# Rotation tables pinned behind the token factor, their loads cut in two, a norm weight moved into its weights, and one product group reordered

## The chip, the cores and the metric

One NeuronCore of a Trainium2 chip runs the kernel. The metric is the device time of one execution in microseconds (us), as the median of several runs. TensorE (PE) multiplies matrices into PSUM banks. VectorE (DVE), ScalarE (ACT) and GpSimd (POOL) do the rest of the arithmetic. SyncE (SP) issues most of the loads and stores (DMAs), POOL some of them. Each engine works through a queue of its own in order; a wait at the head of a queue holds everything behind it.

## What is computed

One decoder layer on 512 tokens of width 1024, all in float32:

```
h  = RMSNorm(x, g_mix);   z = h @ W_in
A  = retention(z) ;  B = 3 groups of dilated window attention(z),
     q and k of each head: RMSNorm with q_gain/k_gain, then rotated by position
x  = x + (sig(g_A) * (A @ W_A) + sig(g_B) * (B @ W_B)) @ W_o
x  = x + relu(RMSNorm(x, g_mlp) @ W_up)^2 @ W_down
x  = x + sig(RMSNorm(x, g_ple) @ W_ple_gate) * (p @ W_ple_proj)
```

The factor of RMSNorm is one number for each token (row) and can be applied after a product; its weight is one number for each column of the left side, that is for each row of the weight matrix.

## The kernel before

**Products in split precision.** Each float32 operand is split into a high part that PE multiplies exactly (hi, made by ACT) and the rest (lo, made by DVE as operand minus hi). A product is three matmuls, hi*hi, hi*lo and lo*hi, into one PSUM bank (`mm3`, L254 to L259). PE therefore has three matmuls of 128x128 by 128x512 for each piece.

**Weights come in units.** `make_plan` (L1088) lists all weights in the order of their use, as units of 512 KB. `fetch` (L179) issues a unit's load on SP into one of six raw buffers; `ahead` (L197) fetches and splits units up to `AHEAD = 2` past those in use, into four pairs of hi and lo buffers; `split_unit` (L214) does the two splits. If a unit has a gain (`g0`), ACT scales by the weight's gain for each row while it makes hi, and DVE makes lo with one scalar_tensor_tensor for each 128 rows; without one, DVE makes it with one subtraction over the whole unit. `units` (L208) hands units to a product.

**The order of the instructions.** The program is traced in the order of the Python code. A scheduler then orders each engine's queue by that order and by times that it assumes for instructions and loads, so an instruction that it takes to be ready early can move ahead of others on its engine. `pin` (L315) ties an instruction behind the one traced before it on the same engine. In the last part of the kernel (`manual_schedule`, L1068 to L1086) ACT and DVE keep the written order. `later` and `tick` (L102, L111) put small work off by a count of product pieces (lag).

**The start.** `setup` (L395) issues the loads of x by columns and of the first four weight units in turn, then of x by rows, then of two more weight units. `load_tables` (L427) then issues the rotation table (`rot_c`, two halves of 512 KB: the first for attention, the second for retention), the attention mask (256 KB) and the q and k gains of all three groups (`rot_gains`, 768 KB, spread over the partitions). `first_panel` (L444) makes q of attention group 0: it splits x and four weight units in turn, then multiplies; in its middle `token_factors` (L503) squares x on ACT, makes v on DVE (L512) and r = v^-0.5 on POOL (L513), and stores r to DRAM and reads it back in another order on SP (L515, L517).

For each of the four tiles of 128 tokens, `consume` (L570) copies the finished bank, times r, to `zn` on ACT (L574), which frees the bank; squares it by heads on ACT (L578), takes a second factor on POOL (L323), applies it on DVE (L580) and rotates (`rotate`, L524) with two table products C and S. `tables` (L555) makes C and S on DVE out of rotation table and gains (L559): two instructions of 128x512 each for q and for k. When four tiles are rotated, PE transposes them by heads (`heads_T`, L545). `embed_operands` (L482) loads p (`praw`) on SP and splits it on ACT (L488) and DVE.

**The MLP.** The hidden width is worked off in four pairs of 512 columns. Each pair's product with `W_down` is a 2x2 block product done with seven block products instead of eight (`seven_gemm`, L923), in the order 4, 3, 5, 4, 3, 5, 2, 2, 1, 1, 7, 7, 6, 6 of half products; each half product uses one unit and takes 12 matmuls. Some units are sums of two weight blocks (a load with an accumulating load on POOL behind it, L194), and the two units of product 1 are differences: DVE subtracts in place (L204) when such a unit is split. The four results are added to x by DVE (`acc`, L945 to L948, line L948) out of the banks; bank 4 is first copied by ACT (L960).

**The embedding gate.** In the last pair, whenever a half of a token tile's x is final (`done`, L950), `gain_T` (L375) multiplies it by `g_ple`, spread over the partitions, on DVE (y, L378), and PE transposes y by four blocks (L333) into a bank; ACT and DVE split that into `h3` hi and lo (L346, L347). When both halves of a tile are there, `mean_squares` (L381) takes its factor, with squares on ACT (L386) and small steps on DVE (L388, L389). Then h3 is multiplied by `W_ple_gate` in two halves of 512 columns, and `fin` (L1077) applies the sigmoid, multiplies by p's projection, adds x and stores.

Of the kernel before, what the change touches and what calls it, by code (L numbers as in the profile page):

```python
# [25 lines left out]
HD = 128  # L26
NG = 3
# [48 lines left out]
class Block:  # L76


    def __init__(self, ctx, tc, a):
        self.tc, self.nc, self.a = tc, tc.nc, a  # L80
        pool = lambda n, b, **k: ctx.enter_context(tc.tile_pool(name=n, bufs=b, **k))
        self.const = pool("const", 1)
        self.wraw = pool("wraw", 6)
        self.wsp = pool("wsp", 4)
        self.bigp = pool("bigp", 16)
        self.tmpp = pool("tmpp", 12)
        self.tabp = pool("tabp", 4)
# [10 lines left out]
        self.hook = None  # L98
        self.plan, self.raws, self.loaded, self.used = [], [], [], 0


# [48 lines left out]

    AHEAD = 2

    def plan_rows(self, w, c0, nk, r0=0):
        for u in range(nk // 2):
            self.plan.append((w[r0 + 256 * u : r0 + 256 * (u + 1), c0 : c0 + 512], None))

    def plan_seven(self, w, r0):


        q = lambda i, j, u: w[r0 + 512 * i + 256 * u : r0 + 512 * i + 256 * (u + 1), 512 * j : 512 * (j + 1)]  # L160
        n = len(self.plan)
        for u in range(2):
            self.plan.append(((q(1, 0, u), q(0, 0, u)), None))
            self.plan.append(((q(0, 1, u), q(1, 1, u)), None))
            self.plan.append((q(1, 1, u), None))
        for u in range(2):
            self.plan.append((q(0, 0, u), None))
        for u in range(2):
            self.plan.append(((None, n + 6 + u, n + 2 + 3 * u), None))
        for u in range(2):  # L170
            self.plan.append(((q(1, 0, u), q(1, 1, u)), None))
        for u in range(2):
            self.plan.append(((q(0, 0, u), q(0, 1, u)), None))
# [23 lines left out]
    def ahead(self, n):  # L197
        while len(self.loaded) < min(len(self.plan), self.used + n):
            i = len(self.loaded)
            self.fetch(i + 1)  # L200
            raw, g0 = self.raws[i]
            src = self.plan[i][0]
            if isinstance(src, tuple) and src[0] is None:
                self.nc.vector.tensor_tensor(raw, raw, self.raws[g0][0], op=ALU.subtract)  # L204
                g0 = None
            self.loaded.append(self.split_unit(raw, g0))

    def units(self, n):  # L208
        self.ahead(n + (0 if self.pinned else self.AHEAD))
# [164 lines left out]

    def gain_T(self, x, t, h, gain, dst, key, lag, bank=None):  # L375

        y = self.tmp("y")
        self.nc.vector.tensor_tensor(y, x[:, h * 512 : (h + 1) * 512], gain[h], op=ALU.mult)  # L378
# [15 lines left out]

    def setup(self):  # L395
        nc, a = self.nc, self.a
        self.gcol = self.const.tile([P, 32], F32, name="gcol")
        nc.scalar.dma_start(self.gcol, a["vec_cols"])
        xr = [self.big("xr") for _ in range(2)]
        self.x_cols = [xr[k // 4][:, k % 4] for k in range(KD)]  # L400
        for u in range(KD // 2):
            src, _ = self.plan[u]
            raw = self.wraw.tile([P, 1024], F32, tag="raw", name=self.nm("raw")).rearrange("p (k n) -> p k n", k=2)
            for k in range(2):
                c = slice((2 * u + k) * P, (2 * u + k + 1) * P)
# [12 lines left out]
        warm = self.tmp("warm")  # L418
        nc.vector.memset(warm, 0.0)
        nc.scalar.activation(warm[:, 500:501], warm[:, 501:502], AF.Copy)  # L420
        wb, wps = warm.bitcast(mybir.dt.bfloat16), self.bank("warm")
        for _ in range(WARM):
            nc.tensor.matmul(wps, wb[:, :P], wb[:, :512], start=True, stop=True)
        self.mhalf = self.const.tile([P, H], F32, name="mhalf")
        nc.gpsimd.memset(self.mhalf, -0.5)

    def load_tables(self):  # L427
        nc, a = self.nc, self.a
        self.rot_c = self.big("rotc")
# [4 lines left out]
        mg = self.big("mg")  # L434
        self.mask = mg[:, 0]
        nc.sync.dma_start(self.mask, a["c_mask"])
        gv = mg.rearrange("p a b -> p (a b)")[:, 512:].rearrange("p (n w) -> p n w", n=4)
        g = a["rot_gains"]
        nc.sync.dma_start(mg.rearrange("p a b -> p (a b)")[:, 512:],
                          bass.AP(tensor=g.tensor, offset=g.offset, ap=[[0, P], [1, 4 * NG * HD]]))  # L440
        self.gains = gv


    def first_panel(self, consume):  # L444
# [110 lines left out]
    def tables(self, g, n):  # L555
        C = self.tabp.tile([P, NT, HD], F32, tag="tab", name=self.nm("C"))
        Sn = self.tabp.tile([P, NT, HD], F32, tag="tab", name=self.nm("S"))
        for o, part, gi in ((C, 0, 2 * n), (Sn, 1, 2 * n + 1)):
            self.nc.vector.tensor_tensor(  # L559
                o, self.rc[:, 0, :, part * HD : (part + 1) * HD],  # L560
                self.gains[:, gi, g * HD : (g + 1) * HD].unsqueeze(1).to_broadcast([P, NT, HD]), op=ALU.mult)
        return C, Sn

    def att_proj(self, g, n):
# [358 lines left out]
    def seven_gemm(self, U, xs, f, ready):  # L923
# [65 lines left out]
    def tail(self, mx):  # L989
# [32 lines left out]
        h3 = None  # L1022
        for f in range(NF // 2):
# [64 lines left out]
    def make_plan(self):  # L1088
# [15 lines left out]
                    self.plan_cols(a["w_up"][0], 512 * (2 * f + b) + 256 * jj, KD)  # L1104
            self.plan_seven(a["w_down"][0], 1024 * f)
        for half in range(2):
            self.plan_rows(a["w_ple_gate"][0], 512 * half, KD)

    def run(self):
        self.w_in = self.a["w_in"][0]  # L1110
        self.make_plan()
        self.setup()
        self.load_tables()
        groups = []
        for g in range(NG):
            groups.append(self.attention(g))
# [7 lines left out]
        assert self.used == len(self.plan) and not self.queue  # L1124


_INS = ["x", "w_in", "g_mlp", "g_ple", "w_ret_out", "w_att_out", "w_o", "w_up", "w_down", "w_ple_proj", "w_ple_gate"]


# [23 lines left out]
```

## Time and profile before

| | |
|---|---|
| median of 3 runs | 1023.94 us (1022.09 to 1024.83) |
| the profiled execution | 1021.85 us |
| its span, first to last instruction | 1020.1 us |
| mean granted PE clock | 0.995 of full speed |
| DMA | 135.37 MB, mean 133 GB/s |

A row of a timeline gives the start and the duration in us, the engine (a q behind it: its queue issues a DMA), the line, the operation, the tile written <- the tiles read, the shape and a count; in brackets stands the engine's idle time before it and what ended it. A row of windows gives for each engine the busy time and (x) the number of instructions; behind them stand the granted PE clock, the share of the DMA engines that was busy and GB/s. A row of waits has who waited <- for whom, then us in total, times and the longest. A row of DMA issues has the count, the size of one and the median us from issue to landing.

### The profile page before, as it was taken

The page shows a single profiled execution, that of the slowest core. Times are in us where ns is not written, and L with a number is a line of the kernel's source. Part 1 is how long each engine was busy: PE and PEld are TensorE (multiplying, and loading weights), DVE is VectorE, ACT ScalarE, POOL GpSimd, SP SyncE. Part 2 cuts the span into 40 slices and gives each one's busy share as a digit, 9 for nine tenths or more (in the row PEclk, how much of TensorE's full clock was granted, in tenths as well). Part 3 has the DMA queues.
Part 4 walks back from the last instruction along what each step waited for, and adds up shares of the span by engine and source line. Part 5 has one row for each costly group of instructions (what it writes and reads, how often), then busy time and mean ns, then how long its engine had stood idle before and what let it go on. Part 6 is the DMA issues. An engine that isn't in the chain of part 4 may idle for free.

```text
span 1020.1 us, 12454 instructions
## 1 busy us (share of the span) xinstructions
PE 1001.6 (98%) x4727; PEld 840.5 (82%) x4727; DVE 620.4 (61%) x895; ACT 452.9 (44%) x853; POOL 86.3 (8%) x92
## 2 busy tenths in 40 slices
PE   9799999999999999999999999999999999999898
PEld 7678879889888788888888888988888888888687
DVE  4688367476579544454443455469467659647863
ACT  7554444554533333433322324464453465355451
POOL 0210011011000000010100100100101001000100
PEclk9899999999999999999999999999999999999999
DMA  9534322223144322223234332559749757965721
GB/s 349 188 103 145 105 83 83 81 86 116 53 153 141 98 90 65 83 73 103 83 103 146 134 102 84 142 135 240 189 116 218 200 144 180 243 154 164 207 71 54
DMA packets 86636, 135.37 MB, mean 133 GB/s; under 512 B 6144, under 2 KB 38192, under 8 KB 86576
## 3 DMA queue, kind: packets, MB, share of 16 engines
q1 hardware_dynamic: 77728, 117.78, 35.9%
q0 software_dynamic: 8704, 16.78, 9.6%
q8 instruction: 37, 0.61, 0.2%
q14 instruction: 23, 0.19, 0.1%
q10 hardware_dynamic: 144, 0.02, 0.0%
HBM read 130.32 MB, written 4.24 MB: 132 GB/s over the span
## 4 chain that ended last, share of the span: by engine, by line
PE 87%; DVE 6%; DMA 3%; ACT 1%; issue 1%; POOL 1%; SPq 0%; ACTq 0%; DVEq 0%; POOLq 0%
PE pg L257 25%; PE pg L258 25%; PE pg L259 25%; PE pb L257 2%; PE pb L259 2%; PE pb L258 2%; DVE wlo L225 1%; PE po L664 1%; DMA mg<-in_rot_gains 1%; PE ph L545 1%; PE pt L333 1%; PE sc L641 1%; DVE x L948 1%; DMA praw<-in_p_cols 1%; PE ry L844 1%
## 5 line engine op out<-in xcount | busy, mean ns | idle before, releaser
L225 DVE TENSOR_TENSOR wlo<-raw,whi 128x1024 fp32r<-128x1024 f32 (+1 forms) x200 | 240.8, 1211 | 103.3 <-ACT whi L224 101.7
L224 ACT ACTIVATE whi<-raw 128x1024 fp32r<-128x1024 f32 (+1 forms) x200 | 205.3, 1032 | 202.8 <-PE pg L259 79.6
L257 PE MATMUL pg<-whi,hh 128*128 128x512 f32 x480 | 199.0, 416 | 5.7 <-ACT zn L574 5.7
L259 PE MATMUL pg<-whi,hl 128*128 128x512 f32 x480 | 188.9, 394 | 0.0
L258 PE MATMUL pg<-wlo,hh 128*128 128x512 f32 x480 | 188.8, 393 | 0.0
L257 PEld LDWEIGHTS pg<-whi,hh 128*128 128x128 f32 x480 | 99.0, 206 | 21.0 <-ACT zn L574 6.5
L259 PEld LDWEIGHTS pg<-whi,hl 128*128 128x128 f32 x480 | 98.5, 205 | 17.2
L258 PEld LDWEIGHTS pg<-wlo,hh 128*128 128x128 f32 x480 | 99.1, 206 | 14.2
L258 PE MATMUL pg<-h2l,whi 128*128 128x512 f32 (+1 forms) x288 | 105.3, 366 | 0.0
L257 PE MATMUL pg<-h2h,whi 128*128 128x512 f32 (+1 forms) x288 | 105.3, 365 | 0.0
L259 PE MATMUL pg<-h2h,wlo 128*128 128x512 f32 (+1 forms) x288 | 105.2, 365 | 0.0
L194 POOL DMA_DIRECT2D raw<-in_w_down x32 | 38.8, 1223 | 323.7 <-DMA raw<-in_w_down 256.6
L323 POOL TENSOR_TENSOR r<-v,mhalf 128x4 f32<-128x4 f32 (+1 forms) x40 | 32.9, 822 | 389.5 <-DVE v L322 389.5
L259 PEld LDWEIGHTS pg<-h2h,wlo 128*128 128x128 f32 x288 | 54.3, 189 | 8.8
L258 PEld LDWEIGHTS pg<-h2l,whi 128*128 128x128 f32 x288 | 54.3, 189 | 8.7
L257 PEld LDWEIGHTS pg<-h2h,whi 128*128 128x128 f32 x288 | 54.3, 189 | 8.6
L258 PE MATMUL pg<-wlo,uh 128*128 128x512 f32 x128 | 50.8, 397 | 2.2 <-DVE wlo L225 2.2
L257 PE MATMUL pg<-hh,whi 128*128 128x512 f32 x128 | 52.4, 409 | 0.0
L259 PE MATMUL pg<-whi,ul 128*128 128x512 f32 x128 | 50.6, 395 | 0.0
L257 PE MATMUL pg<-whi,uh 128*128 128x512 f32 x128 | 50.0, 392 | 0.0
L259 PE MATMUL pg<-hh,wlo 128*128 128x512 f32 x128 | 50.0, 390 | 0.0
L258 PE MATMUL pg<-hl,whi 128*128 128x512 f32 x128 | 49.9, 390 | 0.0
(182 smaller groups left out, 1643.3 us busy)
## 6 DMA issues: line engine op xcount, KB each, us to landing
raw<-in_w_in SPq DMA_DIRECT2D x72, 512.0 KB, 3.9
raw<-in_w_down SPq DMA_DIRECT2D x48, 512.0 KB, 3.7
raw<-in_w_up SPq DMA_DIRECT2D x32, 512.0 KB, 5.1
raw<-in_w_down POOLq DMA_DIRECT2D x32, 512.0 KB, 6.9
x<-in_x SPq DMA_DIRECT2D x8, 512.0 KB, 6.4
raw<-in_w_ret_out SPq DMA_DIRECT2D x8, 512.0 KB, 3.5
raw<-in_w_o SPq DMA_DIRECT2D x8, 512.0 KB, 3.3
raw<-in_w_ple_gate SPq DMA_DIRECT2D x8, 512.0 KB, 4.9
```

The source lines that it names most:

```text
L194: self.nc.gpsimd.dma_start(raw, rows(add[0]), accum_op=ALU.add)
L224: self.pin(nc.scalar.activation(R(hi[:, i]), raw[:, i], AF.Copy))
L225: nc.vector.tensor_tensor(R(lo[:, i]), raw[:, i], hi[:, i], op=ALU.subtract)
L257: t.matmul(ps, sh, mh, start=first, stop=False, skip_group_check=more)
L258: t.matmul(ps, sh, ml, start=False, stop=False, skip_group_check=more)
L259: t.matmul(ps, sl, mh, start=False, stop=last, skip_group_check=more)
L323: self.nc.gpsimd.tensor_tensor(r, v, self.mhalf[:, :w], op=ALU.pow)
L333: nc.tensor.transpose(ps[:, k * P : (k + 1) * P], part[:, k * P : (k + 1) * P], self.ident)
L545: self.nc.tensor.transpose(ps[:, t * P : (t + 1) * P], rots[t][:, h * HD : (h + 1) * HD], self.ident)
L641: nc.tensor.matmul(sc[:, h * P : (h + 1) * P], qT[:, h, rs], kT[:, h, rs], start=True, stop=True)
L664: nc.tensor.matmul(po[:, h * P : (h + 1) * P], v[:, vt, h * HD : (h + 1) * HD], pt, start=b == 0, stop=b == len(blocks) - 1)
L844: nc.tensor.matmul(y, sT[0][:, r], v[:, i, c], start=True, stop=i == 0)
```

## The change

Four edits.

1. The loads of the rotation table and the gains are cut. The first half of the rotation table and the gains of attention group 0 are loaded in `setup`, ahead of the fifth and sixth weight unit; the mask, the other gains and the second half are loaded behind the first projection (`load_rest`). For this the gains are stored group by group.
2. The products of `tables` of group 0, for q and k, are pinned behind the DVE instruction that was traced before them: for q that is the first tile's L580, for k the last addition of the fourth tile's rotation.
3. `g_ple` becomes eight more columns of `gcol`, the gain of the `W_ple_gate` units (`g0=32`), so that `gain_T` transposes x itself in the last pair.
4. In all four pairs the two differences are taken together, behind the split of the unit before them. In the last pair units are split three ahead, the banks of product 1 are taken before product 2, and the first two transposed blocks of h3 go through these banks, with other lags.

```diff
     def ahead(self, n):
-                self.nc.vector.tensor_tensor(raw, raw, self.raws[g0][0], op=ALU.subtract)
                 g0 = None
             self.loaded.append(self.split_unit(raw, g0))
+            for v, w in self.differences.get(i, ()):
+                self.nc.vector.tensor_tensor(self.raws[v][0], self.raws[v][0], self.raws[w][0], op=ALU.subtract)
...
     def plan_seven(self, w, r0):
+        self.differences[n + 7] = [(n + 6 + u, n + 2 + 3 * u) for u in range(2)]
...
     def gain_T(self, x, t, h, gain, dst, key, lag, bank=None):
-        y = self.tmp("y")
-        self.nc.vector.tensor_tensor(y, x[:, h * 512 : (h + 1) * 512], gain[h], op=ALU.mult)
+        y = x[:, h * 512 : (h + 1) * 512]
+        if gain is not None:
+            y = self.tmp("y")
+            self.nc.vector.tensor_tensor(y, x[:, h * 512 : (h + 1) * 512], gain[h], op=ALU.mult)
...
     def setup(self):
-        self.gcol = self.const.tile([P, 32], F32, name="gcol")
+        self.gcol = self.const.tile([P, 40], F32, name="gcol")
...
+        self.load_tables()
         self.fetch(6)
...
     def load_tables(self):
-        for s in range(2):
-            nc.sync.dma_start(rc[:, s], a["c_rot"][s * S : (s + 1) * S].rearrange("(t p) e -> p t e", p=P))
-        nc.sync.dma_start(self.mask, a["c_mask"])
-        nc.sync.dma_start(mg.rearrange("p a b -> p (a b)")[:, 512:],
-                          bass.AP(tensor=g.tensor, offset=g.offset, ap=[[0, P], [1, 4 * NG * HD]]))
+        self.rot_rows(0)
+        self.gain_rows(0, 1)
+
+    def rot_rows(self, s):
+        self.nc.sync.dma_start(self.rc[:, s], self.a["c_rot"][s * S : (s + 1) * S].rearrange("(t p) e -> p t e", p=P))
+
+    def gain_rows(self, g0, g1):
+        g, w = self.a["rot_gains"], 4 * HD
+        self.nc.sync.dma_start(self.gains[:, g0:g1].rearrange("p g n e -> p (g n e)"),
+                               bass.AP(tensor=g.tensor, offset=g.offset + w * g0, ap=[[0, P], [1, w * (g1 - g0)]]))
+
+    def load_rest(self):
+        self.nc.sync.dma_start(self.mask, self.a["c_mask"])
+        self.gain_rows(1, NG)
+        self.rot_rows(1)
...
     def tables(self, g, n):
         for o, part, gi in ((C, 0, 2 * n), (Sn, 1, 2 * n + 1)):
-            self.nc.vector.tensor_tensor(
+            ins = self.nc.vector.tensor_tensor(
...
+            if g == 0:
+                self.tc.keep_in_program_order(ins)
...
     def attention(self, g):
         qT = self.att_proj(g, 0)
+        if g == 0:
+            self.load_rest()
         kT = self.att_proj(g, 1)
...
     def seven_gemm(self, U, xs, f, ready):
-                if first:
+                if first and m != 1:
                     banks[bank, p] = self.gbank() if m in (3, 4) else self.bank("pb")
...
-                ready(2 * i + p, j)
+                ready(2 * i + p, j, banks.get((1, p)))
...
         m4 = []
+        for p in range(2):
+            banks[1, p] = self.bank("pb")
...
     def tail(self, mx):
-        g2, g3 = self.gain_row("g_mlp"), self.gain_row("g_ple")
+        g2 = self.gain_row("g_mlp")
...
-                def ready(t, j):
+                def ready(t, j, free):
                     late = (t < 2) == (j == 0)
-                    self.gain_T(xs[t], t, j, g3, h3, "h3", 0 if late else 5 - 4 * (t // 2),
-                                None if late else self.gbank)
+                    self.gain_T(xs[t], t, j, None, h3, "h3", 0 if late else 1 + t // 2,
+                                None if late else (lambda s: free) if t < 2 else self.gbank)
...
                 order.__enter__()
+                self.AHEAD = 3
             self.seven_gemm(U, xs, f2, ready)
+        self.AHEAD = 2
...
     def make_plan(self):
-            self.plan_rows(a["w_ple_gate"][0], 512 * half, KD)
+            self.plan_rows(a["w_ple_gate"][0], 512 * half, KD, g0=32)
...
     def run(self):
         self.setup()
-        self.load_tables()
```

More of the change, by code (lines that the diff above doesn't have):

```diff
@@ L98, in __init__ @@
         self.hook = None
+        self.differences = {}
         self.plan, self.raws, self.loaded, self.used = [], [], [], 0
@@ L151, with plan_rows @@
     AHEAD = 2
-    def plan_rows(self, w, c0, nk, r0=0):
+    def plan_rows(self, w, c0, nk, r0=0, g0=None):
         for u in range(nk // 2):
-            self.plan.append((w[r0 + 256 * u : r0 + 256 * (u + 1), c0 : c0 + 512], None))
+            self.plan.append((w[r0 + 256 * u : r0 + 256 * (u + 1), c0 : c0 + 512], None if g0 is None else g0 + 2 * u))
     def plan_seven(self, w, r0):
@@ L430, in load_tables @@
         rc = self.rot_c.rearrange("p (s u) (v e) -> p s (u v) e", s=2, v=2)
-        for s in range(2):
-            nc.sync.dma_start(rc[:, s], a["c_rot"][s * S : (s + 1) * S].rearrange("(t p) e -> p t e", p=P))
         self.rc = rc
-        mg = self.big("mg")
-        self.mask = mg[:, 0]
-        nc.sync.dma_start(self.mask, a["c_mask"])
-        gv = mg.rearrange("p a b -> p (a b)")[:, 512:].rearrange("p (n w) -> p n w", n=4)
-        g = a["rot_gains"]
-        nc.sync.dma_start(mg.rearrange("p a b -> p (a b)")[:, 512:],
-                          bass.AP(tensor=g.tensor, offset=g.offset, ap=[[0, P], [1, 4 * NG * HD]]))
-        self.gains = gv
+        self.mg = self.big("mg")
+        self.mask = self.mg[:, 0]
+        self.gains = self.mg.rearrange("p a b -> p (a b)")[:, 512:].rearrange("p (g n e) -> p g n e", g=NG, n=4)
+        self.rot_rows(0)
[10 more added lines that the diff above has]
+        self.rot_rows(1)
     def first_panel(self, consume):
@@ L558, in tables @@
         for o, part, gi in ((C, 0, 2 * n), (Sn, 1, 2 * n + 1)):
-            self.nc.vector.tensor_tensor(
+            ins = self.nc.vector.tensor_tensor(
                 o, self.rc[:, 0, :, part * HD : (part + 1) * HD],
-                self.gains[:, gi, g * HD : (g + 1) * HD].unsqueeze(1).to_broadcast([P, NT, HD]), op=ALU.mult)
+                self.gains[:, g, gi].unsqueeze(1).to_broadcast([P, NT, HD]), op=ALU.mult)
+            if g == 0:
+                self.tc.keep_in_program_order(ins)
         return C, Sn
@@ L1124, in run @@
         assert self.used == len(self.plan) and not self.queue
-_INS = ["x", "w_in", "g_mlp", "g_ple", "w_ret_out", "w_att_out", "w_o", "w_up", "w_down", "w_ple_proj", "w_ple_gate"]
+_INS = ["x", "w_in", "g_mlp", "w_ret_out", "w_att_out", "w_o", "w_up", "w_down", "w_ple_proj", "w_ple_gate"]
 def kernel(**inputs):
@@ L1136 @@
         g = inputs[n][0].reshape(NG, 2, HD // 2)
-        qk += [g.reshape(-1), g[:, ::-1].reshape(-1)]
-    data["rot_gains"] = np.ascontiguousarray(np.concatenate(qk)[None])
+        qk += [g.reshape(NG, HD), g[:, ::-1].reshape(NG, HD)]
+    data["rot_gains"] = np.ascontiguousarray(np.stack(qk, 1).reshape(1, -1))
     data["x_cols"] = np.ascontiguousarray(inputs["x"][0].T)
@@ L1141 @@
     data["vec_cols"] = np.ascontiguousarray(np.concatenate(
-        [inputs[n][0] for n in ("g_mix", "ret_gn", "b_gate")]).reshape(-1, P).T)
+        [inputs[n][0] for n in ("g_mix", "ret_gn", "b_gate", "g_ple")]).reshape(-1, P).T)
     arrays, aps = {}, {}
```

## The prediction

> **What bounds the kernel now.** I read the profile's page first (busy time, the slices), then TensorE's (PE's) waits, its stages by windows, and last the first 70 us and the last 85 us by timeline.
>
> ```profile
> PE 1001.6 (98%) x4727; PEld 840.5 (82%) x4727; DVE 620.4 (61%) x895; ACT 452.9 (44%) x853; POOL 86.3 (8%) x92
> ...
> PE   9799999999999999999999999999999999999898
> ```
>
> PE is the bound: full in all slices but the second and the last four. Only its idle time at the two ends can be won; DVE and ACT matter where PE waits for them. The largest of PE's waits (us in total, times, longest):
>
> ```profile
> PE pg L257 <- ACT zn L574: 5.7, 2, 5.5
> ```
>
> By windows (PE busy, PEld, DVE, ACT, POOL, then the granted clock):
>
> ```profile
> 0.00:20.00 20.00, 18.54 (x71) 13.42 (x72) 11.37 (x17) 15.52 (x25) 0.73 (x7) 1.00 0.94 343
> 20.00:40.00 20.00, 14.49 (x56) 11.53 (x55) 7.97 (x16) 10.12 (x31) 2.96 (x3) 0.83 0.73 245
> ...
> 680.00:720.00 40.00, 40.00 (x178) 33.15 (x177) 34.92 (x39) 17.50 (x18) 4.83 (x4) 1.00 0.86 225
> ...
> 940.00:960.00 20.00, 18.26 (x86) 14.08 (x84) 17.35 (x22) 7.92 (x10) 2.42 (x2) 1.00 0.92 232
> 960.00:980.00 20.00, 17.79 (x78) 14.00 (x77) 17.00 (x28) 11.70 (x25) 2.21 (x4) 0.91 0.35 112
> 980.00:1000.00 20.00, 19.95 (x88) 16.18 (x88) 10.98 (x14) 6.89 (x9) 0.00 (x0) 1.00 0.14 52
> ```
>
> A matmul takes 19.95/88 = 0.227 us at full clock (last row). In 20 to 40 PE loses 5.5 us and some clock; in 940 to 980, with DVE at 17 of 20, it loses 4 us and some clock. The clock by single microseconds:
>
> ```profile
> 31.00:32.00 1.00, 0.00 (x0) 0.00 (x0) 1.00 (x3) 0.00 (x0) 0.29 (x1) 0.50 1.05 389
> ...
> 962.00:963.00 1.00, 0.18 (x1) 0.18 (x2) 1.00 (x2) 0.00 (x0) 0.00 (x0) 0.89 0.00 0
> 963.00:964.00 1.00, 1.00 (x3) 0.81 (x4) 1.00 (x2) 0.00 (x0) 0.00 (x0) 0.50 0.18 39
> ```
>
> PE's two long waits (5.50 and 2.21 us, rows below) each end at half clock.
>
> **The start, part by part.** The timeline, with what each engine waited for in brackets:
>
> ```profile
> 20.80 0.19 ACT L509 ACTIVATION_READ_ACCUMULATOR j<-x 128x1 f32 x1
> 21.23 1.15 ACT L224 ACTIVATE whi<-raw 128x512 fp32r<-128x512 f32 x2 [0.23 <-DMA raw<-in_w_in]
> 22.62 1.15 ACT L224 ACTIVATE whi<-raw 128x512 fp32r<-128x512 f32 x2 [0.24 <-DMA raw<-in_w_in]
> 28.98 0.69 DVE L559 TENSOR_TENSOR C<-rotc,mg 128x512 f32<-128x512 f32 x1 [12.91 <-DMA mg<-in_rot_gains]
> ...
> 31.40 0.16 DVE L512 TENSOR_SCALAR v<-ss 128x4 f32<-128x4 f32 x1
> ...
> 31.71 1.33 POOL L513 TENSOR_TENSOR r<-v,mhalf 128x4 f32<-128x4 f32 x1 [30.40 <-DVE v L512]
> 33.07 0.37 SPq L515 DMA_DIRECT2D r_dram<-r  x1
> 33.08 0.69 ACT L574 ACTIVATE zn<-pg,r 128x512 f32<-128x512 f32 x1 [9.31 <-POOL r L513]
> 33.82 0.79 PE L257 MATMUL pg<-whi,hh 128*128 128x512 f32 x1 [5.50 <-ACT zn L574]
> 37.81 0.40 PE L257 MATMUL pg<-whi,hh 128*128 128x512 f32 x1
> ```
>
> Read it backwards from 33.82. PE has finished the first panel at 33.82 - 5.50 = 28.3; the second panel needs a PSUM bank, and zn, the copy of the first tile on ACT, frees it; zn needs the token factor r, a power on POOL, and that needs v on DVE. The sums for v are there at 21.0 (20.80 + 0.19), but DVE's queue holds the four table products ahead of v, and these wait 12.91 us for the gains. The products take 31.40 - 28.98 = 2.42 us, 0.605 each.
>
> *Pinning the products.* v starts at 21.0, r is ready at 31.71 + 1.33 - 31.40 = 1.64 later, at 22.6. *Reordered loads.* 512 KB of rotation and 256 KB of gains now go ahead of the fifth and sixth weight unit; at 343 GB/s that is 2.3 us, so the last split moves from 22.62 to 24.9 and ends at 26.1. ACT takes zn after it: 26.1 to 26.8, before PE asks at 28.3. So this wait goes, and with it the half clock of 33.82 to 37.81 (4.0 us for 2.0 us of work): PE is 7.5 us early there.
>
> That no load costs more than its bytes is read from 21.23 and 22.62: two 512 KB loads landed 1.4 us apart, which is their bytes at about 375 GB/s. The bound on the other side is among the rivals.
>
> *What is late next.* The same stretch further on:
>
> ```profile
> 53.21 0.68 DVE L535 TENSOR_TENSOR ro<-ro,ro 128x512 f32<-128x512 f32 x1
> 53.81 2.35 DVE L225 TENSOR_TENSOR wlo<-raw,whi 128x1024 fp32r<-128x1024 f32 x2
> ...
> 53.95 0.33 PE L545 MATMUL ph<-ident,ro 128*128 128x128 f32 x1 [1.35 <-DVE ro L535]
> ...
> 56.61 0.46 SPq L486 DMA_DIRECT2D praw<-in_p_cols  x1
> ...
> 63.63 1.06 ACT L488 ACTIVATE pT<-praw 128x1024 fp32r<-128x1024 f32 x1 [6.79 <-DMA praw<-in_p_cols]
> ...
> 66.75 0.50 PE L257 MATMUL pg<-whi,hh 128*128 128x512 f32 x1 [0.17 <-ACT zn L574]
> ```
>
> From the first zn to the fourth rotated tile DVE and POOL work in one chain, 33.08 to 53.89 = 20.8 us. It now starts at 26.1 and holds two products (1.2 us) behind the first tile's norm, where the rotations and the weight splits queue behind them: 48.1. PE, 7.5 us early, reaches the head transposes at 45.1 and waits 3.0 us. There it is 53.95 - 48.2 = 5.7 us ahead, then falls to half clock for about 4 us: 3.7 ahead. Without the clock's fall another bound comes: the p load is issued behind two weight loads that wait for the splits of 53.81; those now end at 48.1 + 1.2 (the other two products, which wait for the fourth tile) + 2.35 = 51.6 instead of 56.2, 4.5 earlier, and ACT holds zn behind that load. So the start brings 3.7 to 4.5; I take 4.0. Ends: 7.5 if both next waits are ordered away, 0 if the loads come in a bad order (below).
>
> The Trainium skill (TensorE: Matmul & The Clock Gate, Part 1: The HAM clock gate) has the clock halved after an idle window of about 3.4 us. By it the 3.0 us wait would leave the clock alone, the start would bring 4.5 and the sum below would be 1015.0. The rows differ: half clock stands at 31.0, 2.7 us after 28.3, and follows 2.21 us at 962.8.
>
> The mask, the other gains and the second rotation half are now written behind the first projection; they have no producer, their bytes are the same, and their first users come after 50 us: nothing. The vector columns grow from 32 to 40:
>
> ```profile
> gcol<-in_vec_cols ACTq DMA_DIRECT2D x1, 16.0 KB, 3.0
> ```
>
> A quarter more of 16 KB is 4 KB, 0.01 us at 343 GB/s, beside x columns and weights that land in the same microseconds: I take 0, at worst 0.1.
>
> **The tail, part by part.**
>
> ```profile
> 938.63 0.69 DVE L378 TENSOR_TENSOR y<-x,gr 128x512 f32<-128x512 f32 x1
> 939.01 0.39 PE L257 MATMUL pg<-whi,uh 128*128 128x512 f32 x1
> 941.49 1.22 DVE L204 TENSOR_TENSOR raw<-raw,raw 128x1024 f32<-128x1024 f32 x1
> 943.91 1.23 DVE L225 TENSOR_TENSOR wlo<-raw,whi 128x1024 fp32r<-128x1024 f32 x1 [1.21 <-ACT whi L224]
> 947.48 1.22 DVE L225 TENSOR_TENSOR wlo<-raw,whi 128x1024 fp32r<-128x1024 f32 x1 [1.21 <-ACT whi L224]
> 950.01 1.40 DVE L948 SCALAR_TENSOR_TENSOR x<-pg,f,x 128x512 f32<-128x512 f32 x2
> 961.55 2.35 DVE L225 TENSOR_TENSOR wlo<-raw,whi 128x1024 fp32r<-128x1024 f32 x2
> 962.82 0.79 PE L258 MATMUL pg<-wlo,uh 128*128 128x512 f32 x1 [2.21 <-DVE wlo L225]
> 965.97 0.16 DVE L388 TENSOR_TENSOR s<-ss 128x1 f32<-128x1 f32 x1 [0.67 <-ACT j L386]
> 970.42 0.89 PE L257 MATMUL pg<-whi,h3h 128*128 128x512 f32 x2
> ```
>
> PE's rest from the second product (939.01) to the gate (970.42) takes 31.4 us; 96 matmuls are 21.8 and six blocks of transposes some 2, so at most 7.5 can be won. DVE sets it, in written order. *Norm weight:* eight y products go. Four stand before 952, 4 x 0.605 = 2.4 us off DVE. The other four only filled the wait for ACT's squares (0.67 left at 965.97): nothing. *Gate weights:* a unit's low part becomes two scalar_tensor_tensor (950.01: 1.40 the pair) instead of 2.35/2 = 1.18; two units lie ahead of the gate: +0.4. *Differences together:* each of the two left DVE idle 1.21 us (943.91, 947.48) for ACT; back to back these hide: 2.4 us. They also release the sixth products' weight buffers some 5 us earlier, so the load behind the 2.21 us wait is no longer late. *Three ahead:* a split waits for the buffer of four products before, which PE has left by then; but two splits more stand ahead of each accumulation, and the copies of bank 4 stand behind a split that waits for the first difference: ready about when PE asks, 0 to 0.5. Transposing into product 1's bank adds a wait of product 1 for the h3 low parts: 0 to 0.5. Sum: -2.4 + 0.4 - 2.4 = -4.4, the ends 0 and -7.5. I take the sum over DVE and not PE's 7.5, since DVE is at 17 of 20 and its written order keeps it from overtaking. PE will still wait somewhere before the gate, where the squares and the extra splits stand ahead of the last h3 parts, so I leave one half-clock stretch in, as now. In the other three pairs PE is full; nothing.
>
> **Sum.** -4.0 - 4.4 = -8.4. The profiled execution took 1021.85 us (span 1020.1), so 1013.45; the median of the runs, 1023.94, stands 2.1 above it: 1015.5.
>
> **Rivals.** *The start is lost:*
>
> ```profile
> r_dram<-r SPq DMA_DIRECT2D x1, 2.0 KB, 10.0
> ```
>
> r comes earlier, so its store of 512 four-byte pieces, 10 us to landing, and the read-back that waits for it on SP may be queued ahead of the next weights. Those then land past 39, where PE needs them (28.3 plus 48 matmuls), with their splits about 45: the start brings 1, total 1018.5. Against: the buffers those weights need are free before the squares end, so SP has them first. The same 1 is left if each of the two loads put ahead of the weights costs, besides its bytes, the 3.0 us that the 16 KB load took to land: the splits then end at 32.1 and zn starts 1.0 before its 33.08. Against: the 1.4 us above. [...] *The tail is lost:* the splits ahead of the accumulations cost what the products gave, total 1019.9. For: written order allows no overtaking. *Neither works*, because other waits take over: 1023.9. *Slower:* in the first three pairs the two subtractions (2.4 us) now stand ahead of the accumulations that free banks 3 and 5. DVE has 5 us in 40 left there (680 to 720). If PE waited 2.4 and fell to half clock (2.0) in each, 3 x 4.4 = 13.2: 1028.7. It decides only from the point where the read of bank 5 is later than its next product, four products or 10.9 us on; little speaks for it.
>
> **How the numbers follow.** Forecast 0.62, start lost 0.11, tail lost 0.17, neither 0.06, slower 0.04. Range 1010.0 (5.7 at the start, 7.5 at the tail, rounded) to 1021.0, past the two one-sided cases. A measurement can tell about 0.3%, 3.07 us, here: the first three cases are faster but for 0.03 of the one-sided ones. Faster 0.87, same 0.09, slower 0.04.
>
> **What would show it.** Right: no wait of PE for zn near 28; v near 21; PE waiting for the rotation L535 near 45 to 48, with a half clock; four y products gone before the gate with DVE free of the two gaps. Wrong: r_dram ahead of weight loads; PE waiting for m, for bank 1, or in the earlier pairs.

## The result, and the profile after

| | before | after |
|---|---|---|
| median of 4 runs each, same chip | 1023.76 us (1022.09 to 1024.83) | 1014.7 us (1013.72 to 1015.35) |
| ratio, 95% interval | | 0.9916 [0.9902, 0.9929] |
| the profiled execution | 1021.85 us | 1015.35 us |
| its span | 1020.1 us | 1013.6 us |
| mean granted PE clock | 0.995 | 0.997 |

The changed kernel is 9.1 us faster by the medians, 6.5 us in the two profiled executions: the one of before is 1.9 us below the median of its kernel, the one of after 0.65 above. The traces explain the 6.5; the rest is taken up under the sum.

PE's waits after (us in total, times, longest):

```profile
PE ph L560 <- DVE ro L550: 4.3, 2, 3.5
PE pt L336 <- DVE x L967: 2.9, 1, 2.9
PE pg L260 <- ACT h3h L349: 1.6, 1, 1.6
```

The wait for zn, 5.5 us before, is no longer in the list. Two others have grown: for the rotation (L550), and in the tail for the last x (L967). The start's timeline after:

```profile
20.52 0.17 DVE L527 TENSOR_SCALAR v<-ss 128x4 f32<-128x4 f32 x1 [4.73 <-ACT j L524]
23.61 2.36 ACT L227 ACTIVATE whi<-raw 128x512 fp32r<-128x512 f32 x4 [3.12 <-DMA raw<-in_w_in]
25.88 0.67 ACT L591 ACTIVATE zn<-pg,r 128x512 f32<-128x512 f32 x1
...
47.49 0.69 DVE L550 TENSOR_TENSOR ro<-ro,ro 128x512 f32<-128x512 f32 x1
...
48.23 0.33 PE L560 MATMUL ph<-ident,ro 128*128 128x128 f32 x1 [3.48 <-DVE ro L550]
...
125.15 1.16 PE L683 MATMUL po<-pT,v 128*128 128x128 f32 x8 [1.09 <-DVE pT L149]
```

v starts when the squares end, zn at 25.88 is ahead of PE, and PE runs on until 48.23 - 3.48 = 44.75. There it waits for DVE's fourth rotated tile. The clock behind this wait, by single microseconds (PE, PEld, DVE, ACT, POOL, then the granted clock):

```profile
48.00:49.00 1.00, 0.77 (x4) 0.69 (x5) 1.00 (x3) 0.41 (x1) 0.00 (x0) 0.99 0.30 43
49.00:50.00 1.00, 1.00 (x4) 0.74 (x3) 1.00 (x2) 0.77 (x2) 0.00 (x0) 0.50 0.86 289
50.00:51.00 1.00, 1.00 (x5) 0.77 (x4) 1.00 (x3) 0.00 (x0) 0.33 (x1) 0.50 0.50 193
51.00:52.00 1.00, 1.00 (x5) 0.90 (x4) 0.19 (x1) 0.00 (x0) 1.00 (x1) 0.50 0.46 49
52.00:53.00 1.00, 1.00 (x5) 0.77 (x5) 0.91 (x2) 0.00 (x0) 0.05 (x1) 0.81 0.80 211
```

What is missing to full clock adds up to 0.01 + 3 x 0.50 + 0.19 = 1.70 us: a stretch of 3.4 us at half clock. The last row of the start's timeline is a convenient mark: this short wait of PE for pT stands in every kernel here, at 129.82 in before:

```profile
129.82 1.16 PE L664 MATMUL po<-pT,v 128*128 128x128 f32 x8 [1.09 <-DVE pT L148]
```

In this pair of executions the start is therefore worth 129.82 - 125.15 = 4.67 us. The tail after:

```profile
931.34 2.35 DVE L209 TENSOR_TENSOR raw<-raw,raw 128x1024 f32<-128x1024 f32 x2
933.77 1.23 DVE L228 TENSOR_TENSOR wlo<-raw,whi 128x1024 fp32r<-128x1024 f32 x1
...
948.35 1.06 ACT L227 ACTIVATE whi<-raw 128x1024 fp32r<-128x1024 f32 x1 [3.42 <-DMA raw<-in_w_down]
949.44 1.23 DVE L228 TENSOR_TENSOR wlo<-raw,whi 128x1024 fp32r<-128x1024 f32 x1 [3.41 <-ACT whi L227]
952.47 1.06 ACT L227 ACTIVATE whi<-raw 128x1024 fp32r<-128x1024 f32 x1 [2.57 <-DMA raw<-in_w_down]
...
956.41 1.41 DVE L233 SCALAR_TENSOR_TENSOR wlo<-raw,gcol,whi 128x512 fp32r<-128x512 f32 x2
957.74 0.75 DVE L967 SCALAR_TENSOR_TENSOR x<-pb,f,x 128x512 f32<-128x512 f32 x1
958.54 0.66 PE L336 MATMUL pt<-ident,x 128*128 128x128 f32 x4 [2.86 <-DVE x L967]
964.02 0.50 PE L260 MATMUL pg<-whi,h3h 128*128 128x512 f32 x1 [1.62 <-ACT h3h L349]
```

The two differences stand together (931.34, x2) with no idle time, the y products are gone, the gate weights' low parts are pairs of scalar_tensor_tensor (956.41). But ACT and DVE now stand still for loads of W_down (948.35, 952.47): the units of product 6. In the written order the last sums into x come behind their splits, at 957.74, and PE waits 2.86 and 1.62 us instead of 2.21. From the mark to the gate's first product it was 970.42 - 129.82 = 840.60 us before and is 964.02 - 125.15 = 838.87 now: in this pair the tail is worth 1.73 us. Behind the gate nothing changes (49.7 and 49.6 to the end). 4.67 + 1.73 + 0.1 = 6.5.

### The profile page after: what moved, and what is told of

The parts are those of the page before. It is cut to its first block, busy times and chain, and to the rows that moved or that the text cites. A ratio compares the mean times of both kernels' runs of the same rounds, so it can differ in the third digit from the quotient of the medians.

```text
span 1013.6 us, 12464 instructions
## 1 busy us (share of the span) xinstructions
PE 998.0 (98%) x4727; PEld 838.1 (83%) x4727; DVE 615.9 (61%) x895; ACT 455.1 (45%) x861; POOL 86.3 (9%) x92
## 4 chain that ended last, share of the span: by engine, by line
PE 89%; DVE 5%; DMA 3%; ACT 1%; issue 1%; SPq 0%; POOL 0%; ACTq 0%; DVEq 0%; POOLq 0%
PE pg L260 26%; PE pg L261 25%; PE pg L262 25%; PE pb L261 2%; PE pb L260 2%; PE pb L262 2%; PE po L683 1%; PE ph L560 1%; DMA raw<-in_w_in 1%; PE sc L660 1%; PE pt L336 1%; DMA raw<-in_w_down 1%; DVE wlo L228 1%; DMA x<-in_x 1%; PE ry L863 1%
## 5 line engine op out<-in xcount | busy, mean ns | idle before, releaser
L228 DVE TENSOR_TENSOR wlo<-raw,whi 128x1024 fp32r<-128x1024 f32 (+1 forms) x192 | 231.5, 1211 | 105.1 <-ACT whi L227 103.3
L227 ACT ACTIVATE whi<-raw 128x1024 fp32r<-128x1024 f32 (+1 forms) x192 | 197.4, 1032 | 204.5 <-PE pg L262 84.8
```

Of the source, the lines that this page charges most:

```text
L227: self.pin(nc.scalar.activation(R(hi[:, i]), raw[:, i], AF.Copy))
L228: nc.vector.tensor_tensor(R(lo[:, i]), raw[:, i], hi[:, i], op=ALU.subtract)
```

## The experiments

Theory: the start gains by the pin, and DVE's rotation is the next limit; the tail gains by the norm weight, while the seven products' part is lost to the late loads of product 6. Rivals: the start gains by the loads; the tail's rest is only DVE's written order.

**The change in its halves.** start_only has edits 1 and 2, tail_only edits 3 and 4, as they stand in the diff above.

> The two edits at the start alone (loads cut, products pinned); the tail as before. By the two traces PE is 4.7 us ahead from 70 us on, so 1023.8 - 4.7 = 1019.1; the prediction's term was 4.0 (1019.8). If the whole 9.1 us of the medians were won at the start: 1014.7.

> The norm weight in the weights and the reordered product group alone; the start as before. The prediction's term was 4.4: 1019.4. By the two traces the stretch from product 2 to the gate became only 1.7 us shorter: 1022.1. The rival that the splits ahead of the accumulations cost what the products gave: 1023.8.

On one chip with a median of before of 1022.2: start_only 1018.61, ratio 0.9962 [0.995, 0.9975], 3.6 us faster; tail_only 1018.49, 0.9964 [0.9952, 0.9977], 3.7 us faster. Each half is worth something alone: the start less than the 4.7 us expected from the traces, the tail more than their 1.7.

**The start in its halves.** pin_only leaves the loads as before:

```diff
     def tables(self, g, n):
-            self.nc.vector.tensor_tensor(
+            ins = self.nc.vector.tensor_tensor(
...
+            if g == 0:
+                self.tc.keep_in_program_order(ins)
```

loads_only is edit 1 without these lines.

> Only the pinning of group 0's table products; loads and tail as before. If v behind the products was the cause, this alone takes PE's wait of 5.5 us away, although the gains still land near 29: v near 21, the first rotation waits for the gains until 29.0 instead of 29.8, so 4 to 5 us faster, 1019 to 1020. If the gains' late landing was the cause, the rotation chain is held and less than 2 us are won: over 1022.

> Only the cut and reordered loads; the products may stand ahead of v again, the tail is as before. The products then run at 22.2 to 24.6, v at 24.6, r at 26.3, zn before PE asks at 28.3: also 4 to 5 us faster, 1019 to 1020. If the order on DVE matters beyond the landing of the gains, PE waits for zn again and it stays over 1021.

Same chip and same runs of before: pin_only 1015.54, 0.9934 [0.9922, 0.9947], 6.7 us faster; loads_only 1017.0, 0.9949 [0.9935, 0.9962], 5.2 us. I had expected 4 to 5 us of either. At the start PE waits for zn at most 0.4 us in each of them, so either edit alone removes the wait of 5.5 us. The pin alone is better than both together (3.6): the intervals do not touch. The loads alone are better by the medians, but their interval overlaps that of start_only. In pin_only:

```profile
23.64 0.67 ACT L576 ACTIVATE zn<-pg,r 128x512 f32<-128x512 f32 x1
...
29.06 0.69 DVE L559 TENSOR_TENSOR C<-rotc,mg 128x512 f32<-128x512 f32 x1 [1.41 <-DMA mg<-in_rot_gains]
...
47.49 0.33 PE L545 MATMUL ph<-ident,ro 128*128 128x128 f32 x1 [2.39 <-DVE ro L535]
```

and in start_only, the same two steps:

```profile
26.22 0.67 ACT L586 ACTIVATE zn<-pg,r 128x512 f32<-128x512 f32 x1
...
48.56 0.48 PE L555 MATMUL ph<-ident,ro 128*128 128x128 f32 x1 [3.49 <-DVE ro L545]
```

768 KB of tables ahead of the last two weight units move their splits, and zn behind them, by 2.6 us, and DVE starts its chain of rotations later. Without the cut DVE waits 1.41 us for the gains, but even so reaches the fourth tile 1.1 us sooner. The rest of the 3.2 us between the two kernels' marks (126.52 and 123.29) is put down to the clock: with PE's wait of 3.49 us in start_only come 6.8 us at half clock, 5.6 of them behind the wait, and with the 2.39 us in pin_only none.

**The tail in its parts.** gate_only is edit 3 alone, group_only edit 4 alone (its transposes take y as before).

> The norm weight alone: the embedding gate's y products are dropped and its norm weight goes into its weights (two scalar_tensor_tensor in a low part's place), nothing else of the change. My theory, term by term: four products of 0.605 less ahead of 952 on DVE, two split halves of 0.2 more, so 2.0 us faster than before (0.998). Rival A, the tail's gain of 3.7 with norm weight and differences together is the norm weight's alone: 0.996. Rival B, the wait for the sixth products' loads sets the end and DVE has room: no change (0.999 to 1.001), the products' time turning into a longer wait of DVE for the late differences.

> The seven products' part alone: differences together, product 1's bank for the first transposes, three units ahead; the y products stay. My theory: the two idle stretches of 1.21 us on DVE go, 2.4 us (0.998), and together with the norm weight alone the 3.7 us of the two in one kernel. Rival A: all of the 3.7 is here (0.996) and the norm weight brings nothing. Rival B: the splits that now stand ahead of the accumulations cost what the gaps gave, no change (0.999 to 1.001), and the traces show bank 4's copies later than before.

On a second chip (before 1023.8): gate_only 1018.32, 0.9947 [0.9935, 0.9959], 5.5 us faster; group_only 1023.48, 0.9997 [0.9988, 1.0007], nothing. The norm weight brings more than my theory (2.0) and its rival A (3.7) said. For the other part rival B came true in the time. The copies of bank 4 do come later, as it said: 3.9 us later than before, reckoned from the marks (939.45 - 130.66 against 934.74 - 129.82). But late_pp, below, has them as late and gains all the same, so they are not the cost. The seven products' part brings nothing by itself, and 3.7 for both parts against 5.5 for the one (on different chips) suggested that it costs something. In group_only's timeline PE waits three times in a row before the gate:

```profile
963.24 0.50 PE L261 MATMUL pg<-wlo,uh 128*128 128x512 f32 x1 [0.84 <-DVE wlo L228]
968.26 0.63 PE L336 MATMUL pt<-ident,y 128*128 128x128 f32 x4 [1.78 <-DVE y L381]
970.24 0.80 PE L260 MATMUL pg<-whi,h3h 128*128 128x512 f32 x1 [1.35 <-ACT h3h L349]
```

With these waits come 6.8 us at half clock (969.1 to 975.9), and the way from the gate to the end takes 1022.4 - 970.24 = 52.2 us for 49.7 before.

**The two late things of after, each taken away.** late_pp asks for pp, the 2 MB of the last projection's weights, later:

```diff
-            if f == NF // 2 - 1:
-                pp = [self.big("pp") for _ in range(2)]
-                for half in range(2):
-                    nc.sync.dma_start(pp[half], ...)
...
             self.seven_gemm(U, xs, f2, ready)
...
+        pp = [self.big("pp") for _ in range(2)]
+        for half in range(2):
+            self.tc.keep_in_program_order(nc.sync.dma_start(pp[half], ...))
```

late_heads lets PE do other products before the first heads:

```diff
-        return self.heads_T(rots, g > 0, 12)
+        return self.heads_T(rots, g > 0, 15 if lazy else 12)
```

> The changed kernel, but the 2 MB of the last projection's weights (pp) are asked for behind the last load of the seven products instead of ahead of the loads of products 5 and 6. My theory, that the sixth products' raw loads landed 7.3 us after their buffers came free (932.59 to 939.85) because they queued behind pp: they land 3 to 4 us earlier, their accumulating loads (now 948.27 and 952.36) likewise, DVE's idle 3.41 at 949.44 shrinks, and the accumulations that wait for those splits come up to 3 us earlier; 2 to 3 us faster than the changed kernel, about 1012. Rival A: the accumulating loads need their 8 to 10 us whatever stands ahead, or DVE's written order sets the end anyway: within 1 us of the changed kernel (1014.7). Rival B: pp comes too late for the last projection and PE waits for it behind the gate: slower than the changed kernel.

> The changed kernel, but the head transposes of the first projection wait three slots longer (15 products behind the projection instead of 12), so that PE has other products while DVE ends the fourth rotation. My theory, that PE's 3.5 us wait for the rotation (48.23) and the half clock behind it (48.9 to 52.8, about 1.9 us) are what the start lost after the weights' wait had gone: both go, up to 5.4 us, less what is late next (zn of the second panel's last tile at 58.87); 2.5 to 5 us faster than the changed kernel, 1010 to 1012.5. Rival A: what stands behind the heads (the second panel's rows, praw landed at 55.99) takes the wait over in full: no change. Rival B: only the half clock goes and the wait moves behind the products put ahead: 2 us faster.

Same chip as gate_only: late_pp 1011.56, 0.9882 [0.9869, 0.9894]; late_heads 1016.62, 0.9925 [0.9912, 0.9939], where the changed kernel has 0.9916 [0.9902, 0.9929]. The issues of DMAs between 930 and 950 (count, size, median us to landing), after:

```profile
raw<-in_w_down SPq DMA_DIRECT2D x2, 512.0 KB, 7.3
raw<-in_w_down POOLq DMA_DIRECT2D x2, 512.0 KB, 9.1
```

and in late_pp:

```profile
pp<-pp_dram SPq DMA_DIRECT2D x2, 1024.0 KB, 10.4
raw<-in_w_down SPq DMA_DIRECT2D x2, 512.0 KB, 3.7
raw<-in_w_down POOLq DMA_DIRECT2D x2, 512.0 KB, 7.9
```

Behind pp product 6's loads took 7.3 us to land, ahead of it 3.7. The accumulating loads behind them, on POOL, took only a little longer with pp ahead (9.1 for 7.9), but they could go out only when those had landed, which is 7.3 us after 932.59 in after:

```profile
940.48 1.20 POOL L196 DMA_DIRECT2D raw<-in_w_down  x1 [11.77 <-DVE h3l L350]
```

and in late_pp:

```profile
937.55 1.20 POOL L196 DMA_DIRECT2D raw<-in_w_down  x1 [7.73 <-DMA raw<-in_w_down]
```

SP's queue shows the order, in before:

```profile
928.68 0.97 SPq L1051 DMA_DIRECT2D pp<-pp_dram  x2
942.73 0.37 SPq L192 DMA_DIRECT2D raw<-in_w_down  x1
```

and in after:

```profile
924.02 0.97 SPq L1072 DMA_DIRECT2D pp<-pp_dram  x2
932.59 1.54 SPq L194 DMA_DIRECT2D raw<-in_w_down  x2
```

Before, 14 us lay between pp's issue and product 6's; now 8.6. DVE's timeline in late_pp no longer has a gap at that place:

```profile
945.33 1.22 DVE L228 TENSOR_TENSOR wlo<-raw,whi 128x1024 fp32r<-128x1024 f32 x1
946.46 0.69 DVE L350 TENSOR_TENSOR h3l<-pt,h3h 128x512 fp32r<-128x512 f32 x1
947.07 1.22 DVE L228 TENSOR_TENSOR wlo<-raw,whi 128x1024 fp32r<-128x1024 f32 x1
...
955.36 0.74 DVE L967 SCALAR_TENSOR_TENSOR x<-pb,f,x 128x512 f32<-128x512 f32 x1
```

From mark to gate it is 835.35, 3.5 us less than after; the ratios give the same 0.0034 of 1023.8, 3.5 us, and their intervals do not touch. The theory holds, with a little more than the 2 to 3 us that it promised. Its rivals fall: the accumulating loads do need nearly their 8 us, but the time does not stay within 1 us of the changed kernel; DVE's written order is the same in both kernels and can't be the difference; PE does not wait for pp behind the gate. late_heads gains nothing. In its timeline PE's wait is gone from 48, and stands at the heads of the next projection:

```profile
72.36 0.47 PE L560 MATMUL ph<-ident,ro 128*128 128x128 f32 x1 [3.25 <-DVE ro L550]
```

with 3.4 us of half clock behind it. That addition of DVE starts at 71.61 in late_heads and at 71.58 in after: DVE's chain of rotations runs through from zn to here, and what PE gains before it, it waits for here. Of what I expected the first rival came true, by another bound than the one that it named.

**The combinations.** To see which parts are worth keeping, four kernels without the cut loads: pin_gate (pin and norm weight), pin_tail (pin and edits 3 and 4), and each with pp late.

> Before with the four rotation products of the first group pinned (no loads split or moved) and with the norm weight in the gate's weights; the seven products as before. If the parts add up, 6.7 + 5.5 = 12.2 us faster than before (0.988), faster than the changed kernel with only two of its four parts. Rival: the two parts share a half-clock stretch in the tail (pin_only had none there), so that they give less together: 10.4 us (0.990).

> As pin_gate, with the seven products' part of the change (differences together, product 1's bank, three units ahead) as well: the changed kernel without its split and moved loads. Theory: this part makes the sixth products' loads meet the load of pp, and costs what it gives, so nothing is won over pin_gate, or up to 1.8 us are lost (the difference of norm weight alone, -5.5, and both, -3.7): 0.988 to 0.990. Rival, the differences' two gaps of 1.2 us come off on top of the norm weight: 2.4 us faster than pin_gate (0.986). Against the changed kernel (0.9916) it shows the split loads alone: 3.1 us at the start by the earlier runs.

> As pin_gate, with pp asked for behind the last load of the seven products. Theory: in the order of before the sixth products' buffers come free after pp has landed, so nothing queues behind it and the move brings nothing: within 0.7 us of pin_gate. Rival: the accumulating loads of products 4 and 5 gain from it too: 1 to 3 us faster than pin_gate.

> As pin_tail, with pp asked for behind the last load of the seven products. Theory: here the move brings what it brought to the changed kernel, 3 to 3.5 us over pin_tail, and only now the seven products' part is worth something, 1.5 to 2.5 us over pin_gate_pp: about 14 us faster than before (0.986). Rival: DVE's written order is the end with or without the loads; the same as pin_gate_pp within 0.7 us.

On a third chip (before 1022.24):

| | median, us | ratio, 95% interval |
|---|---|---|
| pin_gate | 1012.78 | 0.9903 [0.9888, 0.9918] |
| pin_gate_pp | 1012.17 | 0.9899 [0.9884, 0.9914] |
| pin_tail | 1012.58 | 0.9903 [0.9888, 0.9917] |
| pin_tail_pp | 1010.35 | 0.9879 [0.9862, 0.9895] |

The single parts do not add up to 12.2 in pin_gate: it brings 9.5 us, nearer to the rival's 10.4. The seven products' part brings 0.2 with pp early and 1.8 with pp late; moving pp brings 0.6 without that part and 2.2 with it. That is what I had expected of pin_tail and pin_gate_pp; pin_tail_pp is 11.9 us faster than before and not 14, and its step over pin_tail is 2.2 and not 3 to 3.5. The intervals of the four ratios overlap, but all four runs of pin_tail_pp (1009.01 to 1010.79) lie below all runs of the other three (from 1011.3). The marks of the profiles, in us, show where the differences lie; each is one execution:

| kernel | mark | mark to gate | half clock, start / tail |
|---|---|---|---|
| before | 129.82 | 840.60 | 6.8 / 3.4 |
| tail_only | 128.75 | 838.19 | 6.8 / 3.4 |
| gate_only | 128.68 | 837.50 | 3.4 / 0 |
| group_only | 130.66 | 839.58 | 6.8 / 6.8 |
| start_only | 126.52 | 840.05 | 6.8 / 0 |
| after | 125.15 | 838.87 | 3.4 / 0 |
| late_heads | 125.50 | 838.33 | 3.4 / 3.4 |
| late_pp | 126.29 | 835.35 | 3.4 / 0 |
| loads_only | 123.86 | 840.81 | 0 / 3.4 |
| pin_only | 123.29 | 840.06 | 0 / 0 |
| pin_gate | 123.76 | 837.44 | 3.4 / 0 |
| pin_gate_pp | 123.38 | 838.22 | 3.4 / 3.4 |
| pin_tail | 122.11 | 837.98 | 0 / 0 |
| pin_tail_pp | 123.54 | 835.40 | 3.4 / 0 |

(The last column sums the stretches at half clock, in us, from windows of 1 us, as long as PE has matmuls.) The rows fall into groups; rows of one group differ by up to 2.0 us in the start and 0.9 in the tail. *Start, by the mark:* untouched 129.5 (mean of four), pin and cut loads 125.9 (four), pin without the cut 123.2 (five), cut without the pin 123.9 (one). *Tail, mark to gate:* untouched 840.4 (four), norm weight alone 837.7 (three), with the seven products' part 838.3 (four), with that and pp late 835.4 (two). So the pin alone is worth 6.3 us and the cut takes 2.7 of them back, about 1 us of that through more time at half clock. The norm weight is worth 2.7. The seven products' part brings nothing on top as long as pp is early (0.6 more, within the rows' spread), and 2.3 to 2.8 when pp is late (1.8 by the timing). Alone, in group_only, it shortens the way to the gate by 0.8 us (839.58), and the 52.2 us behind the gate take more than that back. The best of the kernels is pin_tail_pp.

## Why the prediction was right, point by point

The forecast was -8.4 in two terms and 1015.5 us; the median came out at 1014.7. The sign, the size and the mechanism of the start held. One step of the tail failed.

*Start, pinning the products.* Right: v at 20.52 for 21.0, zn at 25.88 for 26.1, no wait of PE at 28. *What is next late.* Right: DVE's fourth tile; PE was there at 44.75 (45.1 predicted) and waited 3.48 us (3.0), then ran at half clock for 3.4 us (4). The term was -4.0; the profiled pair shows -4.67, the four profiles of the edits together -3.6, the timing of them alone -3.6. Right too that the second panel's rows would not hold PE: there is no wait for them in the list. *Reordered loads.* Priced rightly as their bytes (2.3 us predicted, 2.6 measured between pin_only and start_only), but I took the two edits as one, and never asked what the pin would do with the loads as they were. It does more: the gains landed only 1.4 us too late for it. The wait for zn would have gone without the cut. *The rival of the start* did not come: the store of r went out behind weight loads,

```profile
20.66 3.48 SPq L194 DMA_DIRECT2D raw<-in_w_in  x3
24.77 0.63 SPq L530 DMA_DIRECT2D r_dram<-r  x1
```

and the one load that went out behind it, at 27.57, made PE wait for nothing before 44.75. No load was charged 3 us beside its bytes. The Trainium skill (DMA: Bandwidth & Descriptors, Anatomy of one DMA — SWDGE (gpsimd) path) states a fixed cost of about 2.0 us for a DMA on GpSimd's path. These two loads are issued by SP, and no such cost shows for them: 26.1 + 2 x 2.0 would be an estimate of zn at 30.1, and the trace has 25.88.

*Tail, norm weight.* Right in kind: -2.4 + 0.4 = -2.0 predicted, -2.7 by the marks. Here the difference between marks and timing is large (5.5 alone); see below.

*Tail, differences together.* This is the step that failed. The two idle stretches of 1.21 us did go, and the buffers of product 6 did come free earlier: its loads went out at 932.59 and not at 942.73, which is 5.5 us earlier when reckoned from the mark, as predicted (5). But "the load behind the 2.21 us wait is no longer late" was wrong. The release came so early that the load fell behind pp, 8.6 us after pp's issue, where pp takes 9.9 us to land (median in after), and not 14 us after it. The load took 7.3 us, its accumulating load landed at 948.3, and DVE lost 3.41 us there, more than the two gaps. I had not asked what the queue holds that the released load enters. late_pp and the pair pin_gate_pp and pin_tail_pp show that pp was what stood in the way: with it gone the term is -2.3 to -2.8 by the marks and -1.8 by the timing (-2.4 predicted); with pp early it is nothing. The rival "the tail is lost" was thus half right, by another mechanism than the written order that it named. That the splits ahead and the wait for product 1's bank would cost 0 to 0.5 each was right, so far as PE's list has no wait for that bank.

*The other three pairs.* Right. A late mark is the copy ur on ACT that waits 3.37 us, in before:

```profile
917.45 0.60 ACT L1029 ACTIVATE ur<-pg 128x512 f32<-128x512 f32 x1 [3.37 <-PE pg L259]
```

and in after:

```profile
912.78 0.60 ACT L1050 ACTIVATE ur<-pg 128x512 f32<-128x512 f32 x1 [3.37 <-PE pg L262]
```

From the first mark to this one it is 917.45 - 129.82 = 787.63 us before and 912.78 - 125.15 = 787.63 after. The rival that ends slower has no place there.

*The sum.* By the marks start and tail together are -3.6 - 2.0 = -5.6, in the profiled pair -6.5, by the medians -9.1, and by the two halves timed alone -7.3. The forecast stands between these, and its closeness to the median is partly luck: the tail's term (-4.4) came out at half its size, by the marks. Before itself was timed at 1022.2 to 1023.8 on different chips. The ratios' intervals are 1.3 us to each side, so 9.1 and 7.3 are not told apart. Where the rest of the 9.1 lies isn't settled, since only one execution of each kernel is profiled. Stretches at half clock are one candidate: for before the mean clock of a run varied from 0.992 to 0.997, for after from 0.997 to 0.998, and 3.4 us of half clock are 0.0017 of it. But the 33 executions of before that were timed beside the experiments speak against more than a small part: the nine with a clock of 0.997 are on average 1.1 us faster than the five with 0.992 or 0.993 (each against the median of its chip), though 4.5 us of PE's work lie between these clocks.

## What to carry to other kernels

Before an edit that releases a buffer earlier, look at what is in flight on the DMA queues at the new time, not at the old one: a load that is due later, moved behind it, can be worth more than the edit. Where two edits remove the same wait, price each alone; the one that only reorders an engine's queue may do, and the other then costs its bytes for nothing. And before shifting work away from a wait, find the next place where the same chain of the other engine is awaited: PE's 3.5 us at 48 came back as 3.25 us at 72.

## What the runs showed of the hardware

The stretches at half clock come in lumps: in all fourteen profiles, in the start and in the tail, they add up to 0, 3.4 or 6.8 us, so at most 1.7 or 3.4 us of work lost; what falls into the wait itself costs nothing (2.9 of the 6.8 us in before, 30.9 to 33.8). All eight waits of 3.25 us and more had one or two lumps. Whether one follows a wait is not decided by the wait's length between 2 and 3 us: the 2.39 us of pin_only at 47.49 and the 2.86 us of after at 958.54 were followed by none, the 1.95 us of pin_gate at 46.77 by a full one. PE's row there, and the windows behind it:

```profile
46.77 0.33 PE L547 MATMUL ph<-ident,ro 128*128 128x128 f32 x1 [1.95 <-DVE ro L537]
```

The granted clock is the column behind POOL:

```profile
47.00:48.00 1.00, 1.00 (x6) 0.76 (x6) 1.00 (x3) 0.86 (x2) 0.00 (x0) 0.88 0.58 96
48.00:49.00 1.00, 1.00 (x4) 0.70 (x3) 1.00 (x2) 0.32 (x1) 0.00 (x0) 0.50 1.00 377
49.00:50.00 1.00, 1.00 (x6) 1.00 (x5) 0.73 (x3) 0.00 (x0) 0.79 (x1) 0.50 0.14 51
50.00:51.00 1.00, 1.00 (x4) 0.71 (x4) 0.37 (x1) 0.00 (x0) 0.60 (x1) 0.50 0.53 111
51.00:52.00 1.00, 1.00 (x7) 0.82 (x6) 1.00 (x3) 0.00 (x0) 0.00 (x0) 0.92 0.93 289
```

(0.12 + 3 x 0.50 + 0.08 = 1.70.) The Trainium skill (TensorE: Matmul & The Clock Gate, Part 1: The HAM clock gate) has the clock decided in a window of about 3.4 us that runs freely of the kernel. The length of the lumps agrees with that, and so does the chance in it: the same wait may or may not bring a lump. That a full window of idleness is needed does not agree: 1.95 us were enough here. So the term for a wait of about 2 us should be its length and then 0 or 1.7 us. In the tail a lump cost less: with it (before, loads_only, pin_gate_pp) the way from mark to gate was 0.5 to 0.8 us longer than without (start_only, pin_only, pin_gate). Those three have a wait of PE for the last h3 parts at the gate (0.76, 0.76 and 1.05 us), the others have none: PE, slowed by the clock, came no earlier than these parts.
